# Plain float32 for the memory projection, tokens prepared at twice the pace beside it, and another product order in the first output pair

## The chip, the cores and the metric

One core of one Trainium2 chip runs the whole layer. The metric is device time in microseconds (us) of one execution. Matrix products run on PE (TensorE); DVE is VectorE, ACT ScalarE, POOL GpSimd, SP the engine that issues the DMAs. All code lines report as line 48 (a helper that records every operation), so the rows are told apart by the names of their tiles.

## The reference, cut to what matters

```python
h = rms_norm(x, norm_g[l])                       # x: 512 tokens x 2048
proj = h @ w_in[l]                               # 2048 x 13312: q, k, v, gates, ...
...
mkv = rms_norm(mem, mem_norm_g[l]) @ w_mem_kv[l] # mem: 256 x 2048, w: 2048 x 1024
mk, mv = jnp.split(mkv, 2, axis=-1)
...                                              # three branches, gated and summed
x = x + merged @ w_out[l]                        # 2048 x 2048
```

Everything is float32.

## The kernel before, in words

**Steps.** The program is a list of steps that run_steps (line 120) writes out in order. A step of a projection is one weight chunk of 256 rows by 512 columns. In each turn i, run_steps issues in this order: the loads of step i+6 (on SP), the "adds" of step i (on DVE), the split of step i+2, the products of step i (on PE) with what follows them (post), the work registered for i with at_step, work put off by after, and small tasks with a budget per step. Every engine works its own queue in this order, so an instruction that waits holds up all that stand behind it on its engine.

**The split.** A float32 product is made of three products in the rounded type fp32r: a tile is divided into a high part (ACT casts it) and a low part (DVE subtracts), and products (line 194) adds high by high, high by low and low by high. split_w (line 183) does it for weights. Its buffers are three deep, so the split for step i+2 waits until PE is through with step i-1.

**Memory's projection** (kv_steps, line 409): 16 steps, each two chunk rows by two tiles of 128 memory tokens, 12 products of 512 columns a step. The memory is turned by PE (mem_piece, line 346; 8 transposes a call pair), scaled by DVE, cast by ACT, and POOL makes the low part.

**The tokens** are normed beside those steps: x_norm (line 502) squares four pieces on ACT, makes 1/rms on DVE (with a power on POOL) and scales the pieces on DVE and ACT; x_turn (line 510) turns them on PE and scales them into blocks on DVE.

**Pairs.** Every pair of 512-column slabs after that (pair, line 232) is one Strassen-Winograd product of 2x2 blocks: seven block products P1 to P7 instead of eight, four steps of 12 products each. Their left operands are made once by class Blocks (line 458): copies of blocks (A11, A12, A22), sums of blocks (s1 to s4) and their split forms (S1 to S4). Each of these is one DVE operation of 128x1024 per half, and a split has an ACT cast before it. H are the blocks of the normed tokens (used by the 13 pairs from q on), M those of the merged branches (used by the two output pairs). The right operands are chunks and differences of chunks (sub, line 244, one DVE operation each, in adds). The order is that of line 229: P1, P5, P6, P3, P7, P2, P4. evac (line 253) adds the finished products up on DVE.

Steps 0 to 15 are the memory's, 16 to 43 the q pair's (P1 16 to 19, P5 20 to 23, P6 24 to 27). Before: the tokens' tile t is normed at step 6+3t and turned in the two steps after; A11 is split at 12 and 13, A12 at 18 and 19, s1 to S4 made at 17 to 25, A22 at 29 and 30 (lines 517 to 525). The second to last lines of the schedule (855 to 859) do the same for M, against the first step n_o of the output pair.

Of the kernel before, what the change touches and what calls it, by code (L numbers as in the profile page):

```python
# [65 lines left out]
def trunk_layer(ctx: ExitStack, tc, x, mem, gx, gm, w_in, w_kv, bg, cw, hg, relz, w_a, w_b, w_m, w_o, out):  # L66
# [160 lines left out]


    ORDER = ("P1", "P5", "P6", "P3", "P7", "P2", "P4")
    LEFT = {"P1": "A11", "P5": "S1", "P6": "S2", "P3": "S4", "P7": "S3", "P2": "A12", "P4": "A22"}  # L230

    def pair(name, left, w, done, bias=None):


        n = NK // 2 // KB
        s0 = len(steps)
        raw, ps, cs, st8 = {}, {}, {}, {}
# [15 lines left out]
        def evac(p):  # L253
            b = ps[key[p]]
            new = lambda what: [cell(f"{what}_{name}{t}") for t in range(2)]
            if p == "P1":
                if bias is None:
                    cs["a"] = cs["b"] = new("pa")
                    for t in range(2):
                        ACT.copy(cs["a"][t], b[t])  # L260
                else:
                    cs["a"], cs["b"] = new("pa"), new("pb")
                    for t in range(2):
                        DVE.tensor_tensor(cs["a"][t], b[t], bias_of(0), op=ALU.add)
                        DVE.tensor_tensor(cs["b"][t], b[t], bias_of(1), op=ALU.add)
            if p == "P5":
                cs["f"] = new("pf")
                for t in range(2):
                    DVE.tensor_tensor(cs["f"][t], b[t], cs["b"][t], op=ALU.add)
            if p == "P6":  # L270
                cs["e"] = new("pe") if bias is None else cs["b"]
                for t in range(2):
                    DVE.tensor_tensor(cs["e"][t], b[t], cs["b"][t], op=ALU.add)
            if p == "P3":
                for t in range(2):
                    DVE.tensor_tensor(cs["e"][t], b[t], cs["e"][t], op=ALU.add)
                done(1, 0, cs["e"])
            if p == "P7":
                for t in range(2):
                    DVE.tensor_tensor(cs["f"][t], b[t], cs["f"][t], op=ALU.add)  # L280
                done(1, 2, cs["f"])
            if p == "P2":
                cs["g"] = new("pg")
                for t in range(2):
                    DVE.tensor_tensor(cs["g"][t], b[t], cs["a"][t], op=ALU.add)
                done(0, 0, cs["g"])
            if p == "P4":
                for t in range(2):
                    DVE.tensor_tensor(cs["a"][t], b[t], cs["a"][t], op=ALU.add)
                done(0, 2, cs["a"])  # L290

        for p in ORDER:
            for c in range(n):
                def do_split(p=p, c=c):
                    st8["w", p, c] = split_w(raw[source[p], c], f"{name}_{p}_{c}")

                def mm(p=p, c=c):
                    k = key[p]
                    if k not in ps:
                        ps[k] = [bank(f"ps{k}_{name}_{t}") for t in range(2)]  # L300
                    hi, lo = left(LEFT[p])
                    opens = p in ("P1", "P5", "P6", "P2")

                    def acts(kk, t):
                        kt, ts = c * KB + kk, slice(t * P, (t + 1) * P)
                        return hi[:, kt, ts], lo[:, kt, ts]

                    products(ps[k], st8["w", p, c], acts, opens and c == 0, c == n - 1, not opens)

                st = Step(mm, do_split)  # L310
                if c == n - 1:
                    st.post.append(lambda p=p: evac(p))
                steps.append(st)

        for c in range(n):
            steps[s0 + c].loads.append(loader("11", 0, 0, c))
            steps[s0 + 1 + c].loads.append(loader("12", 0, 1, c))
            steps[s0 + 7 + c].loads.append(loader("22", 1, 1, c))
            steps[s0 + 19 + c].loads.append(loader("21", 1, 0, c))
            steps[s0 + c].adds.append(sub("11", "12", "11", c))  # L320
            steps[s0 + 5 + c].adds.append(sub("11", "22", "11", c))
            steps[s0 + (10, 12, 14, 16)[c]].adds.append(sub("12", "22", "12", c))
            steps[s0 + (20, 21, 22, 24)[c]].adds.append(sub("21", "21", "11", c))
        if bias is not None:
            def load_bias():
# [1 line left out]
            steps[s0].loads.append(load_bias)  # L327


    S_OF = {"A11": (0, 1), "S1": (2, 3), "S2": (4, 5), "S4": (6, 7), "S3": (8, 9), "A12": (10, 11), "A22": (12, 13)}  # L330

    def piece(dst, src, t, j):
        SP.dma_start(dst[:, j, :], src[t * P:(t + 1) * P, j * S:(j + 1) * S])

    SP.dma_start(gm_sb, gm)
    mraw = [slot(t, f"mem{t}") for t in range(NMT)]
    xraw = [slot((13, 9, 8, 6)[t], f"x{t}") for t in range(NT)]
    mT = []

# [5 lines left out]

    def mem_piece(t, k4):
        if not mT:
            for i in range(4):
                mT.append(slot((4, 5, 10, 11)[i], f"mT{i}", (P, 8, MEM), F32R))
        pt = bank(f"pt_mem{t}_{k4}", (P, 4, P))  # L350
        for j in range(4):
            PE.transpose(pt[:, j, :], mraw[t][:, k4, j * P:(j + 1) * P], ident)
        hs = cell(f"hs_mem{t}_{k4}", (P, 4, P))
        DVE.tensor_tensor(hs, pt, gm_sb[:, 4 * k4:4 * k4 + 4].unsqueeze(2).broadcast_to([P, 4, P]), op=ALU.mult)
        i, j, ts = k4 // 2, (k4 % 2) * 4, slice(t * P, (t + 1) * P)
        hi, lo = mT[i][:, j:j + 4, ts], mT[2 + i][:, j:j + 4, ts]
        ACT.copy(hi, hs)
        POOL.tensor_tensor(lo, hs, hi.bitcast(F32), op=ALU.subtract)

    def mem_rstd(t):  # L360
        row_rstd(squares(mraw[t], f"mem{t}"), f"mem{t}", rm[t])

    def act_mem(k, t):
        ts = slice(t * P, (t + 1) * P)
        return mT[k // 8][:, k % 8, ts], mT[2 + k // 8][:, k % 8, ts]


    def heads_out(name, cells, t0, gcol, dst):
# [40 lines left out]
    def kv_steps():  # L409
        st = {"ps": {}}  # L410
        for c in range(NK // KB):
            for half in range(2):
                def do_load(c=c, half=half):
                    st["raw", c, half] = load(w_kv[c * KB * P:(c + 1) * KB * P, half * S:(half + 1) * S], f"kv{half}_{c}")

                def do_split(c=c, half=half):
                    st["w", c, half] = split_w(st["raw", c, half], f"kv{half}_{c}")

                def mm(c=c, half=half):
                    if c == 0:  # L420
                        st["ps"][half] = [bank(f"ps_kv{half}_{t}") for t in range(NMT)]
                    products(st["ps"][half], st["w", c, half], lambda kk, t: act_mem(c * KB + kk, t),
                             c == 0, c == NK // KB - 1)

                s = Step(mm, do_split)
                s.loads.append(do_load)
                if c == NK // KB - 1:
                    def post(half=half):
# [13 lines left out]

    for j in range(1, 4):
        steps[j - 1].loads.append(lambda j=j: first_loads(j))
    steps[3].loads.append(lambda: [SP.dma_start(d, s) for d, s in ((gx_sb, gx), (hg_sb, hg), (cw_sb, cw))])
    for i in range(16):
        steps[4 + 3 * i // 4].loads.append(lambda i=i: piece(xraw[i // 4], x, i // 4, i % 4))

    for k4 in range(4):
        at_step(-3 if k4 == 0 else 2 * k4 - 2, lambda k4=k4: [mem_piece(t, k4) for t in range(NMT)])  # L450
        if k4 == 0:
            at_step(-3, lambda: None)
    for t in range(NMT):
        at_step(8 + t, lambda t=t: mem_rstd(t))
    at_step(5, lambda: DVE.tensor_scalar_mul(qg, hg_sb, float(DH) ** -0.5))


# [39 lines left out]
        def left(self, b):  # L497
            return self.at[b]

    H = Blocks("h", S_OF, {(0, 0): 12, (0, 1): 13, (1, 0): 7, "S12": 9, "S4": 8})  # L500

    def x_norm(t):
        r = row_rstd(squares(xraw[t], f"x{t}"), f"x{t}")
# [11 lines left out]
                          gx_sb[:, 4 * k4:4 * k4 + 4].unsqueeze(2).broadcast_to([P, 4, P]), op=ALU.mult)  # L515

    for t in range(NT):
        b = 6 + 3 * t
        at_step(b, lambda t=t: x_norm(t))
        at_step(b + 1, lambda t=t: [x_turn(t, 0), x_turn(t, 1)])  # L520
        at_step(b + 2, lambda t=t: [x_turn(t, 2), x_turn(t, 3)])
    for i in range(2):
        for n, what in ((12 + i, "A11"), (17, "s1"), (17, "S1"), (19, "s2"), (20, "s4"), (21, "S2"), (22 + i, "S4"),
                        (23, "s3"), (24 + i, "S3"), (18 + i, "A12"), (29 + i, "A22")):
            at_step(n, lambda i=i, what=what: H.do(what, i))

    def w_pair(src, c0, c1=None):
# [286 lines left out]
    def branch(br, n, src, nk, names, first, end):  # L814
# [10 lines left out]
        def done(t, ps):  # L825
# [7 lines left out]
            if end is not None:  # L833
# [3 lines left out]
        steps[s0 + 1].loads.append(get_g)  # L837


    M = Blocks("m", {"A11": (4, 5), "S1": (0, 1), "S2": (12, 13), "S4": (2, 3), "S3": (10, 7), "A12": (9, 8),  # L840
                     "A22": (6, 11)}, {(0, 0): 10, (0, 1): 11, (1, 0): 6, "S12": 7, "S4": 8})

    def m_turn(n, t):
        pt = bank(f"pt_m{n}_{t}", (P, 4, P))
# [7 lines left out]
        branch("m", n, w_m, HM, ("ym",), False, None)  # L852
        branch("b", n, w_b, HB, ("yb0", "yb1"), False, m_turn)
    n_o = len(steps)
    for n, what, i in ((-7, "A11", 0), (-6, "A11", 1), (-2, "s1", 0), (1, "S1", 0), (1, "s1", 1), (1, "S1", 1),
# [3 lines left out]
        at_step(n_o + n, lambda what=what, i=i: M.do(what, i))  # L859


    def out_pair(i):
# [14 lines left out]
                SP.dma_start(xs[half, t], x[t * P:(t + 1) * P, ns])  # L877

        s0 = len(steps)
        pair(f"o{i}", M.left, w_pair(w_o, 2 * S * i), done)  # L880
        for n, args in ((15, (1, 0)), (19, (1, 2)), (23, (0, 0)), (27, (0, 2))):
            steps[s0 + n].loads.append(lambda args=args: get_x(*args))

# [43 lines left out]
```

## Time and profile before

| what | us |
|---|---|
| median of 3 runs (lowest, highest) | 1560.79 (1557.6, 1560.88) |
| the profiled execution's own time | 1558.05 |
| its span, from the first to the last instruction | 1556.3 |
| PE busy | 1487.0 (96%) |
| DVE busy | 1172.2 (75%) |
| ACT busy | 731.0 (47%) |
| mean granted clock of PE | 0.988 of full speed |

All times in the rows are us from the span's start. A matmul's busy time is longer than its distance to the next one, because matmuls overlap; distances of starts are used for sums. "Idle before" stands in square brackets with what ended it.

### The profile page before, as it was taken

The numbers are of one execution on the slowest core, as the hardware profiler recorded it, in microseconds if no ns is written. First come the engines' busy times: TensorE is split into PE (matmuls) and PEld (weight loads), VectorE is DVE, ScalarE is ACT, GpSimd is POOL, SyncE is SP. The second block draws the span as 40 slices with busy tenths as digits, with TensorE's granted clock in tenths as the row PEclk, the third lists the DMA queues.
The fourth block names the chain that finished last, engine by engine and source line by source line (L and its number), as shares of the span: only waits on it lengthen the run. The fifth ranks groups of instructions, "written<-read, shape, count | busy, mean of one in ns | idle before, by whom it ended". The sixth has DMA issues, their size and how long they took to land. (4 is left out here: it accounts for less than half of the span.)

```text
span 1556.3 us, 18174 instructions
## 1 busy us (share of the span) xinstructions
PE 1487.0 (96%) x6760; PEld 1222.1 (79%) x6760; DVE 1172.2 (75%) x1409; ACT 731.0 (47%) x1125; POOL 32.2 (2%) x31
## 2 busy tenths in 40 slices
PE   7868999999999999999999999999898999998998
PEld 6656888888778888788888888888677888877786
DVE  5688777777788887787878787878567455469987
ACT  4855666644435455444353435444366222234442
POOL 2000000000000000000000000000000000000000
PEclk9989999999999999999999999999998999999999
DMA  9513425362425253525252526266654454611633
GB/s 344 181 43 95 149 75 183 95 216 85 126 75 193 89 178 87 157 81 193 97 201 94 203 93 209 83 218 246 203 164 147 152 189 156 208 56 43 214 122 95
DMA packets 125368, 227.18 MB, mean 146 GB/s; under 512 B 9056, under 2 KB 22368, under 8 KB 124512
## 3 DMA queue, kind: packets, MB, share of 16 engines
q1 hardware_dynamic: 125280, 226.02, 44.3%
q8 instruction: 53, 0.87, 0.2%
q14 instruction: 35, 0.29, 0.1%
HBM read 195.58 MB, written 33.03 MB: 147 GB/s over the span
## 5 line engine op out<-in xcount | busy, mean ns | idle before, releaser
L48 ACT CAST whi_o_P<-raw_o 128x1024 fp32r<-128x1024 f32 x56 | 58.7, 1053 | 87.7 <-DVE raw_o L48 20.9
L48 DVE TENSOR_TENSOR wlo_ga_P<-raw_ga,whi_ga_P 128x1024 fp32r<-128x1024 f32 x56 | 68.5, 1224 | 31.2 <-ACT whi_ga_P L48 30.9
L48 ACT CAST whi_ga_P<-raw_ga 128x1024 fp32r<-128x1024 f32 x56 | 58.9, 1052 | 70.1 <-PE psY_ga L48 22.8
L48 ACT CAST whi_gm_P<-raw_gm 128x1024 fp32r<-128x1024 f32 x56 | 58.9, 1052 | 69.2 <-PE psY_gm L48 22.8
L48 ACT CAST whi_gb_P<-raw_gb 128x1024 fp32r<-128x1024 f32 x56 | 58.9, 1052 | 69.2 <-PE psY_gb L48 22.8
L48 DVE TENSOR_TENSOR wlo_gm_P<-raw_gm,whi_gm_P 128x1024 fp32r<-128x1024 f32 x56 | 68.5, 1224 | 29.7 <-ACT whi_gm_P L48 29.6
L48 DVE TENSOR_TENSOR wlo_gb_P<-raw_gb,whi_gb_P 128x1024 fp32r<-128x1024 f32 x56 | 68.5, 1224 | 29.7 <-ACT whi_gb_P L48 28.2
L48 DVE TENSOR_TENSOR wlo_o_P<-raw_o,whi_o_P 128x1024 fp32r<-128x1024 f32 x56 | 68.3, 1223 | 20.1 <-ACT whi_o_P L48 19.9
L48 PE MATMUL ps_wb<-whi_wb,yb_hi 128*128 128x512 f32 x128 | 49.8, 389 | 0.0
L48 PE MATMUL ps_wb<-wlo_wb,yb_hi 128*128 128x512 f32 x128 | 49.8, 389 | 0.0
L48 PE MATMUL ps_wb<-whi_wb,yb_lo 128*128 128x512 f32 x128 | 49.8, 389 | 0.0
L48 ACT CAST whi_cx_P<-raw_cx 128x1024 fp32r<-128x1024 f32 x28 | 29.5, 1055 | 42.4 <-PE psY_cx L48 13.2
L48 DVE TENSOR_TENSOR wlo_cx_P<-raw_cx,whi_cx_P 128x1024 fp32r<-128x1024 f32 x28 | 34.3, 1224 | 18.9 <-ACT whi_cx_P L48 18.6
L48 PE MATMUL ps_kv<-whi_kv,mT 128*128 128x512 f32 x128 | 44.0, 413 | 2.4 <-ACT whi_kv L48 2.4
L48 ACT CAST whi_bz_P<-raw_bz 128x1024 fp32r<-128x1024 f32 x28 | 29.5, 1052 | 33.3 <-PE psZ_bz L48 11.2
L48 DVE TENSOR_TENSOR wlo_mqz_P<-raw_mqz,whi_mqz_P 128x1024 fp32r<-128x1024 f32 x28 | 34.2, 1223 | 14.2 <-ACT whi_mqz_P L48 14.1
L48 ACT CAST whi_mqz_P<-raw_mqz 128x1024 fp32r<-128x1024 f32 x28 | 29.4, 1051 | 31.4 <-PE psZ_mqz L48 10.0
L48 ACT CAST whi_wb<-raw_wb 128x1024 fp32r<-128x1024 f32 x16 | 16.9, 1055 | 58.0 <-DVE g_m L48 17.5
L48 DVE TENSOR_TENSOR wlo_v_P<-raw_v,whi_v_P 128x1024 fp32r<-128x1024 f32 x28 | 34.1, 1222 | 12.9 <-ACT whi_v_P L48 12.7
L48 DVE TENSOR_TENSOR wlo_bz_P<-raw_bz,whi_bz_P 128x1024 fp32r<-128x1024 f32 x28 | 34.2, 1223 | 12.8 <-ACT whi_bz_P L48 12.6
L48 DVE TENSOR_TENSOR wlo_k_P<-raw_k,whi_k_P 128x1024 fp32r<-128x1024 f32 x28 | 34.0, 1222 | 12.2 <-ACT whi_k_P L48 12.1
L48 DVE TENSOR_TENSOR wlo_az_P<-raw_az,whi_az_P 128x1024 fp32r<-128x1024 f32 x28 | 34.1, 1222 | 11.8 <-ACT whi_az_P L48 11.5
(684 smaller groups left out, 4740.5 us busy)
## 6 DMA issues: line engine op xcount, KB each, us to landing
raw_ga<-in_w_in SPq DMA_DIRECT2D x32, 512.0 KB, 4.9
raw_gb<-in_w_in SPq DMA_DIRECT2D x32, 512.0 KB, 5.0
raw_gm<-in_w_in SPq DMA_DIRECT2D x32, 512.0 KB, 5.4
raw_o<-in_w_o SPq DMA_DIRECT2D x32, 512.0 KB, 6.7
raw_kv<-in_w_kv SPq DMA_DIRECT2D x16, 512.0 KB, 8.1
raw_q<-in_w_in SPq DMA_DIRECT2D x16, 512.0 KB, 7.3
raw_k<-in_w_in SPq DMA_DIRECT2D x16, 512.0 KB, 5.0
raw_v<-in_w_in SPq DMA_DIRECT2D x16, 512.0 KB, 4.5
```

The lines of the kernel that those rows point to most:

```text
L48: ins = getattr(self.engine, op)(*args, **kwargs)
```

## The change

Memory's projection leaves out the split: the turned memory is written in float32 by DVE alone, the weights are multiplied as loaded, 4 plain float32 products of 512 columns a step instead of 12 in fp32r. The casts on ACT, the subtractions on DVE and the low parts on POOL of that stage are gone. A weight buffer is now released by PE instead of by the split.

The pieces of x are loaded two a step from step 3 on (before three in four steps from step 4); tile t is normed at step 2+2t and turned at 3+2t and 4+2t. The blocks follow: A11 at 6 and 7, A12 at 8 and 9, s1 at 11, s3 12, S3 13, S1 14, s2 15, s4 16, S4 17 and 18, S2 19 and 20, A22 22 and 23. The squares of the memory move from steps 8 and 9 to 9 and 10. Buffers are laid out anew to fit.

The first output pair takes the products in the order EARLY: P1, P7, P5, P6, P3, P2, P4. S3, which P7 needs, comes from the first two column slabs only. The differences of the right operands and the sums in evac follow; one pair of DVE additions of 128x512 comes on top. The second output pair and the 13 others keep their order.

```diff
+    EARLY = ("P1", "P7", "P5", "P6", "P3", "P2", "P4")
@@ evac
             if p == "P6":
+                cs["e"] = cs["d"] if early else new("pe") if bias is None else cs["b"]
                 for t in range(2):
+                    DVE.tensor_tensor(cs["e"][t], b[t], cs["d" if early else "b"][t], op=ALU.add)
+                if early:
+                    for t in range(2):
+                        DVE.tensor_tensor(cs["f"][t], b[t], cs["f"][t], op=ALU.add)
+                    done(1, 2, cs["f"])
+            if p == "P7" and early:
+                cs["d"] = new("pd")
+                for t in range(2):
+                    DVE.tensor_tensor(cs["d"][t], cs["b"][t], b[t], op=ALU.subtract)
@@ loads and adds of a pair
+            steps[s0 + (2 if early else 7) + c].loads.append(loader("22", 1, 1, c))
+            if early:
+                steps[s0 + 1 + c].adds.append(sub("12", "22", "12", c))
+                steps[s0 + (8, 9, 10, 12)[c]].adds.append(sub("11", "22", "11", c))
+            else:
+                steps[s0 + 5 + c].adds.append(sub("11", "22", "11", c))
+                steps[s0 + (10, 12, 14, 16)[c]].adds.append(sub("12", "22", "12", c))
@@ mem_piece
-        hs = cell(f"hs_mem{t}_{k4}", (P, 4, P))
-        DVE.tensor_tensor(hs, pt, gm_sb[:, 4 * k4:4 * k4 + 4].unsqueeze(2).broadcast_to([P, 4, P]), op=ALU.mult)
...
-        ACT.copy(hi, hs)
-        POOL.tensor_tensor(lo, hs, hi.bitcast(F32), op=ALU.subtract)
+        j = (k4 % 2) * 4
+        DVE.tensor_tensor(mT[k4 // 2][:, j:j + 4, t * P:(t + 1) * P], pt,
+                          gm_sb[:, 4 * k4:4 * k4 + 4].unsqueeze(2).broadcast_to([P, 4, P]), op=ALU.mult)
@@ kv_steps
-                    products(st["ps"][half], st["w", c, half], lambda kk, t: act_mem(c * KB + kk, t),
-                             c == 0, c == NK // KB - 1)
-                s = Step(mm, do_split)
+                    for k in range(c * KB, (c + 1) * KB):
+                        for t, ps in enumerate(st["ps"][half]):
+                            PE.matmul(ps, mT[k // 8][:, k % 8, t * P:(t + 1) * P], st["raw", c, half][:, k % KB, :],
+                                      start=k == 0, stop=k == NK - 1)
+                s = Step(mm)
@@ the schedule beside memory's steps
-        steps[4 + 3 * i // 4].loads.append(lambda i=i: piece(xraw[i // 4], x, i // 4, i % 4))
+        steps[3 + i // 2].loads.append(lambda i=i: piece(xraw[i // 4], x, i // 4, i % 4))
-        at_step(-3 if k4 == 0 else 2 * k4 - 2, lambda k4=k4: [mem_piece(t, k4) for t in range(NMT)])
+        at_step((-3, 0, 3, 5)[k4], lambda k4=k4: [mem_piece(t, k4) for t in range(NMT)])
-        at_step(8 + t, lambda t=t: mem_rstd(t))
+        at_step(9 + t, lambda t=t: mem_rstd(t))
-        b = 6 + 3 * t
+        b = 2 + 2 * t
-        for n, what in ((12 + i, "A11"), (17, "s1"), (17, "S1"), (19, "s2"), (20, "s4"), (21, "S2"), (22 + i, "S4"),
-                        (23, "s3"), (24 + i, "S3"), (18 + i, "A12"), (29 + i, "A22")):
+        for n, what in ((6 + i, "A11"), (8 + i, "A12"), (11, "s1"), (12, "s3"), (13, "S3"), (14, "S1"), (15, "s2"),
+                        (16, "s4"), (17 + i, "S4"), (19 + i, "S2"), (22 + i, "A22")):
@@ the blocks of the output pairs, and the first of these
+    for n, what, i in ((-7, "A11", 0), (-6, "A11", 1), (-2, "s1", 0), (-1, "s3", 0), (1, "s1", 1), (1, "s3", 1),
+                       (0, "S3", 0), (2, "S3", 1), (3, "S1", 0), (4, "S1", 1), (5, "s2", 0), (5, "s2", 1),
+                       (7, "s4", 0), (8, "s4", 1), (9, "S2", 0), (10, "S2", 1),
+                       (12, "S4", 0), (13, "S4", 1), (16, "A12", 0), (17, "A12", 1), (20, "A22", 0), (21, "A22", 1)):
-        pair(f"o{i}", M.left, w_pair(w_o, 2 * S * i), done)
+        pair(f"o{i}", M.left, w_pair(w_o, 2 * S * i), done, order=ORDER if i else EARLY)
```

## Rows read from the trace of the kernel before

**Rows 1.** The page, part 1: busy time, share of the span, instructions.

```profile
PE 1487.0 (96%) x6760; PEld 1222.1 (79%) x6760; DVE 1172.2 (75%) x1409; ACT 731.0 (47%) x1125; POOL 32.2 (2%) x31
```

**Rows 2.** PE's waits, 0 to 72 us: total, times, longest (us).

```profile
PE pt_x L48 <- DVE x L48: 5.6, 2, 4.6
```

**Rows 3.** PE's waits, 72 to 157 us.

```profile
PE psY_q L48 <- DVE wlo_q_P L48: 5.7, 3, 3.9
PE psZ_q L48 <- ACT whi_q_P L48: 5.0, 1, 5.0
PE psZ_q L48 <- DVE wlo_q_P L48: 3.3, 2, 1.8
```

**Rows 4.** PE in order of time: start, busy us; first product of memory, P1, P3, P7.

```profile
9.39 0.79 PE L48 MATMUL ps_kv<-whi_kv,mT 128*128 128x512 f32 x1 [2.38 <-ACT whi_kv L48]
...
72.05 0.39 PE L48 MATMUL psX_q<-whi_q_P,hA_hi 128*128 128x512 f32 x1
...
134.74 0.39 PE L48 MATMUL psZ_q<-whi_q_P,hS_hi 128*128 128x512 f32 x1
...
145.62 0.39 PE L48 MATMUL psY_q<-whi_q_P,hS_hi 128*128 128x512 f32 x1
```

**Rows 5.** Stretches: busy PE, PEld, DVE, ACT, POOL; granted clock; DMA share, GB/s.

```profile
28.00:32.00 4.00, 4.00 (x23) 3.41 (x22) 2.22 (x4) 2.17 (x3) 1.75 (x2) 1.00 1.05 385
...
100.00:104.00 4.00, 3.39 (x8) 2.67 (x9) 4.00 (x5) 4.00 (x9) 0.00 (x0) 0.53 0.00 0
...
1167.00:1177.00 10.00, 10.00 (x72) 8.66 (x71) 6.47 (x25) 7.26 (x24) 0.00 (x0) 1.00 0.02 6
```

**Rows 6.** PE in order of time, attention: one float32 product of 512 columns.

```profile
1164.01 1.02 PE L48 MATMUL psc_b<-k,q 128*128 128x512 f32 x2
1164.87 0.38 PE L48 MATMUL ptp_b<-ident,p_b 128*128 128x128 f32 x2
```

**Rows 7.** PE in order of time, memory's stage: eight transposes and what follows.

```profile
58.18 1.04 PE L48 MATMUL pt_x<-ident,x 128*128 128x128 f32 x8
58.97 0.48 PE L48 MATMUL ps_kv<-whi_kv,mT 128*128 128x512 f32 x1
```

**Rows 8.** Groups of PE's weight loads in attention: busy us, mean ns.

```profile
L48 PEld LDWEIGHTS psc_b<-k,q 128*128 128x128 f32 x64 | 10.3, 202 | 0.1
```

**Rows 9.** DVE in order of time: start, busy us, idle before.

```profile
7.05 0.69 DVE L48 TENSOR_TENSOR hs_mem<-pt_mem,gm_sb 128x512 f32<-128x512 f32 x1 [0.41 <-PE pt_mem L48]
...
36.02 0.16 DVE L48 TENSOR_REDUCE ss_x<-ss_x 128x1 f32<-128x4 f32 x1 [0.93 <-ACT junk L48]
...
37.80 0.88 DVE L48 TENSOR_SCALAR x<-x,r_x 128x512 f32<-128x512 f32 x2
...
85.11 0.16 DVE L48 TENSOR_SCALAR v_mk<-ss_mk 128x8 f32<-128x8 f32 x1
...
87.79 1.22 DVE L48 TENSOR_TENSOR raw_q<-raw_q,raw_q 128x1024 f32<-128x1024 f32 x1
...
91.26 1.22 DVE L48 TENSOR_TENSOR hf_S<-hf,hf 128x1024 f32<-128x1024 f32 x1
...
98.20 1.22 DVE L48 TENSOR_TENSOR raw_q<-raw_q,raw_q 128x1024 f32<-128x1024 f32 x1
```

**Rows 10.** ACT in order of time: the first of a tile's four squares.

```profile
33.00 0.63 ACT L48 ACTIVATE junk<-x 128x512 f32<-128x512 f32 x1
```

**Rows 11.** The chain that ended last, at the first output pair: start, length.

```profile
1388.51 1.22 DVE raw_o L48
...
1444.55 1.14 DVE raw_o L48
1445.69 1.15 DVE wlo_o_P L48
1446.87 5.51 PE psY_o L48 x23
1452.39 10.99 PE psV_o L48 x48
```

More of the change, by code (lines that the diff above doesn't have):

```diff
@@ L229, in trunk_layer, with pair @@
     ORDER = ("P1", "P5", "P6", "P3", "P7", "P2", "P4")
+    EARLY = ("P1", "P7", "P5", "P6", "P3", "P2", "P4")
     LEFT = {"P1": "A11", "P5": "S1", "P6": "S2", "P3": "S4", "P7": "S3", "P2": "A12", "P4": "A22"}
-    def pair(name, left, w, done, bias=None):
+    def pair(name, left, w, done, bias=None, order=ORDER):
+        early = order is EARLY
         n = NK // 2 // KB
@@ L270, in evac @@
             if p == "P6":
-                cs["e"] = new("pe") if bias is None else cs["b"]
+                cs["e"] = cs["d"] if early else new("pe") if bias is None else cs["b"]
                 for t in range(2):
-                    DVE.tensor_tensor(cs["e"][t], b[t], cs["b"][t], op=ALU.add)
+                    DVE.tensor_tensor(cs["e"][t], b[t], cs["d" if early else "b"][t], op=ALU.add)
[3 more added lines that the diff above has]
+                    done(1, 2, cs["f"])
             if p == "P3":
@@ L277, in evac @@
                 done(1, 0, cs["e"])
-            if p == "P7":
+            if p == "P7" and early:
+                cs["d"] = new("pd")
+                for t in range(2):
+                    DVE.tensor_tensor(cs["d"][t], cs["b"][t], b[t], op=ALU.subtract)
+            elif p == "P7":
                 for t in range(2):
@@ L290, in evac @@
                 done(0, 2, cs["a"])
-        for p in ORDER:
+        for p in order:
             for c in range(n):
@@ L301, in mm @@
                     hi, lo = left(LEFT[p])
-                    opens = p in ("P1", "P5", "P6", "P2")
+                    opens = p in ("P1", "P5", "P2", "P7" if early else "P6")
                     def acts(kk, t):
@@ L317, in pair @@
             steps[s0 + 1 + c].loads.append(loader("12", 0, 1, c))
-            steps[s0 + 7 + c].loads.append(loader("22", 1, 1, c))
+            steps[s0 + (2 if early else 7) + c].loads.append(loader("22", 1, 1, c))
             steps[s0 + 19 + c].loads.append(loader("21", 1, 0, c))
             steps[s0 + c].adds.append(sub("11", "12", "11", c))
-            steps[s0 + 5 + c].adds.append(sub("11", "22", "11", c))
-            steps[s0 + (10, 12, 14, 16)[c]].adds.append(sub("12", "22", "12", c))
+            if early:
[4 more added lines that the diff above has]
+                steps[s0 + (10, 12, 14, 16)[c]].adds.append(sub("12", "22", "12", c))
             steps[s0 + (20, 21, 22, 24)[c]].adds.append(sub("21", "21", "11", c))
@@ L327, in pair @@
             steps[s0].loads.append(load_bias)
-    S_OF = {"A11": (0, 1), "S1": (2, 3), "S2": (4, 5), "S4": (6, 7), "S3": (8, 9), "A12": (10, 11), "A22": (12, 13)}
+    S_OF = {"A11": (0, 1), "A12": (10, 11), "S3": (2, 3), "S1": (6, 8), "S4": (7, 12), "S2": (4, 5), "A22": (9, 13)}
     def piece(dst, src, t, j):
@@ L335, in trunk_layer @@
     SP.dma_start(gm_sb, gm)
-    mraw = [slot(t, f"mem{t}") for t in range(NMT)]
+    mraw = [slot(2 + t, f"mem{t}") for t in range(NMT)]
     xraw = [slot((13, 9, 8, 6)[t], f"x{t}") for t in range(NT)]
@@ L347, in mem_piece @@
         if not mT:
-            for i in range(4):
-                mT.append(slot((4, 5, 10, 11)[i], f"mT{i}", (P, 8, MEM), F32R))
+            for i in range(2):
+                mT.append(slot(4 + i, f"mT{i}", (P, 8, MEM)))
         pt = bank(f"pt_mem{t}_{k4}", (P, 4, P))
@@ L352, in mem_piece @@
             PE.transpose(pt[:, j, :], mraw[t][:, k4, j * P:(j + 1) * P], ident)
-        hs = cell(f"hs_mem{t}_{k4}", (P, 4, P))
-        DVE.tensor_tensor(hs, pt, gm_sb[:, 4 * k4:4 * k4 + 4].unsqueeze(2).broadcast_to([P, 4, P]), op=ALU.mult)
-        i, j, ts = k4 // 2, (k4 % 2) * 4, slice(t * P, (t + 1) * P)
-        hi, lo = mT[i][:, j:j + 4, ts], mT[2 + i][:, j:j + 4, ts]
-        ACT.copy(hi, hs)
-        POOL.tensor_tensor(lo, hs, hi.bitcast(F32), op=ALU.subtract)
+        j = (k4 % 2) * 4
+        DVE.tensor_tensor(mT[k4 // 2][:, j:j + 4, t * P:(t + 1) * P], pt,
+                          gm_sb[:, 4 * k4:4 * k4 + 4].unsqueeze(2).broadcast_to([P, 4, P]), op=ALU.mult)
     def mem_rstd(t):
         row_rstd(squares(mraw[t], f"mem{t}"), f"mem{t}", rm[t])
-    def act_mem(k, t):
-        ts = slice(t * P, (t + 1) * P)
-        return mT[k // 8][:, k % 8, ts], mT[2 + k // 8][:, k % 8, ts]
     def heads_out(name, cells, t0, gcol, dst):
@@ L414, in do_load @@
                     st["raw", c, half] = load(w_kv[c * KB * P:(c + 1) * KB * P, half * S:(half + 1) * S], f"kv{half}_{c}")
-                def do_split(c=c, half=half):
-                    st["w", c, half] = split_w(st["raw", c, half], f"kv{half}_{c}")
                 def mm(c=c, half=half):
@@ L444, in trunk_layer @@
         steps[j - 1].loads.append(lambda j=j: first_loads(j))
-    steps[3].loads.append(lambda: [SP.dma_start(d, s) for d, s in ((gx_sb, gx), (hg_sb, hg), (cw_sb, cw))])
+    steps[2].loads.append(lambda: [SP.dma_start(d, s) for d, s in ((gx_sb, gx), (hg_sb, hg), (cw_sb, cw))])
     for i in range(16):
-        steps[4 + 3 * i // 4].loads.append(lambda i=i: piece(xraw[i // 4], x, i // 4, i % 4))
+        steps[3 + i // 2].loads.append(lambda i=i: piece(xraw[i // 4], x, i // 4, i % 4))
     for k4 in range(4):
-        at_step(-3 if k4 == 0 else 2 * k4 - 2, lambda k4=k4: [mem_piece(t, k4) for t in range(NMT)])
-        if k4 == 0:
-            at_step(-3, lambda: None)
+        at_step((-3, 0, 3, 5)[k4], lambda k4=k4: [mem_piece(t, k4) for t in range(NMT)])
     for t in range(NMT):
-        at_step(8 + t, lambda t=t: mem_rstd(t))
+        at_step(9 + t, lambda t=t: mem_rstd(t))
     at_step(5, lambda: DVE.tensor_scalar_mul(qg, hg_sb, float(DH) ** -0.5))
@@ L498, in left @@
             return self.at[b]
-    H = Blocks("h", S_OF, {(0, 0): 12, (0, 1): 13, (1, 0): 7, "S12": 9, "S4": 8})
+    H = Blocks("h", S_OF, {(0, 0): 12, (0, 1): 13, (1, 0): 7, "S12": 9, "S4": 13})
     def x_norm(t):
@@ L837, in branch @@
         steps[s0 + 1].loads.append(get_g)
-    M = Blocks("m", {"A11": (4, 5), "S1": (0, 1), "S2": (12, 13), "S4": (2, 3), "S3": (10, 7), "A12": (9, 8),
-                     "A22": (6, 11)}, {(0, 0): 10, (0, 1): 11, (1, 0): 6, "S12": 7, "S4": 8})
+    M = Blocks("m", {"A11": (4, 5), "S3": (2, 3), "S1": (0, 1), "S2": (12, 13), "S4": (10, 11), "A12": (9, 7),
+                     "A22": (6, 8)}, {(0, 0): 10, (0, 1): 11, (1, 0): 6, "S12": 7, "S4": 8})
     def m_turn(n, t):
@@ L854, in trunk_layer @@
     n_o = len(steps)
-    for n, what, i in ((-7, "A11", 0), (-6, "A11", 1), (-2, "s1", 0), (1, "S1", 0), (1, "s1", 1), (1, "S1", 1),
[3 rows of a table removed]
+    for n, what, i in ((-7, "A11", 0), (-6, "A11", 1), (-2, "s1", 0), (-1, "s3", 0), (1, "s1", 1), (1, "s3", 1),
[3 rows of a table added]
         at_step(n_o + n, lambda what=what, i=i: M.do(what, i))
```

3 rows, old and new, of the table n_o are left out of this document.

## The prediction

> **What bounds the kernel now.** I read the page first: PE is busy 96% of the span [rows 1], so a change counts only where PE waits or where its own work grows. Then PE's waits by stretch. From 157 us to the attention they are few; they lie in two places that this change touches. In memory's stage they are small and come from the tokens' chain on DVE [rows 2]. In the q pair's first three products they are 14.0 us for splits of weights alone [rows 3]; there DVE works without a break (4.00 of 4.00 in [rows 5]), because the tokens' blocks and the weights' splits stand in one queue. Third, PE's starts [rows 4]: the memory's first product is at 9.39, P1 at 72.05, the fourth product (P3) at 134.74, the fifth at 145.62. So a product takes 10.88 undisturbed (2.72 a step, 0.227 a matmul of 512 columns), and P1, P5 and P6, with 32.6 of work, took 62.7. Fourth, the chain that ended last: at the first output pair it runs over DVE from 1388.51 to 1446.87, and over PE after that [rows 11].
>
> **Memory's stage on PE.** Removed: 192 matmuls x 0.227 = 43.6 us. Added: 64 float32 products of 512 columns. The trace has them in attention: start to next start 0.86 us, two passes each [rows 6], at a granted clock of 1.00 where PE is full [rows 5]. 64 x 0.86 = 55.0, so 3.44 a step. The transposes stay: eight cost 0.79 [rows 7], eleven such sets after the first (three of memory, eight of x) cost 8.7. The stage can start when DVE has scaled the first memory pieces, at 7.05 + 0.69 = 7.7 [rows 9], without ACT's cast and split before it (9.39 so far). After a wait of 5.0 [rows 3] the granted clock over 100 to 104 us is 0.53 [rows 5], so PE is at the lower of its two levels (1.2 GHz) for some 4 us, which costs 1.9; I take that once, for the start (0 to 4 is possible). For x's first tile I take a wait of 1.0 (0 to 3): it needs 5.8 MB to be there (memory 2.1, five weight chunks 2.6, itself 1.05), 15 us at the 385 GB/s that the queues reach [rows 5] and some 4 us to start, then 3.0 us of squares on ACT (33.00 to 36.02 [rows 9, 10]) and 2.7 on DVE (36.02 to 38.68 [rows 9]); PE wants it at some 25. Sum: 7.7 + 55.0 + 1.9 + 8.7 + 1.0 = 74.3, against 72.05. On PE the stage alone loses 2.3.
>
> A float32 product loads its weights twice, 202 ns a load [rows 8], well inside a pass of 0.43, so I add nothing for loads. The Trainium skill (TensorE: Matmul & The Clock Gate, Weight-path perf modes) says that the fast weight load is on only where the type isn't FP32, which speaks against the change; by it the loads would come into the open, and the sum would be that of rival 4. That the attention's products follow each other without a gap is against it.
>
> **What hides at nothing.** All of the stage's loads are 14.7 MB, 38 us at 385 GB/s, under 66 us of PE work; a chunk's buffer is now freed by PE and not by the split, so the thirteenth chunk waits for step 0, twelve steps ahead of its use. On SP the pieces of x stand behind their step's chunk and ahead of later chunks, 1 MB a step, 2.7 us, against PE's 3.44; if that cover went, PE would wait the difference. The three small vectors move ahead of one chunk. POOL's eight subtractions had nobody waiting who isn't removed with them. In the output pair the twelve chunks of the three right blocks fill the ring of twelve buffers in both versions; only their order of use changes.
>
> **The tokens beside it, on DVE.** With steps 11 to 15 free of transposes, PE is through with x's last turn at 74.3 - 17.2 = 57.1, and with step 8's at 48.6. DVE then scales two turned pieces (1.4) and norms tile 3 (2.7): 52.6. Now the memory's norms are ahead in the queue: ACT casts a half of A12 (1.0) and makes the squares (3.0) to 56.6; DVE takes 1.8 to 1/rms (36.02 to 37.80), 1.4 for x's pieces, 1.1 for A12: 60.9; the second memory tile's squares are done at 60.6, so 1.8 and 1.4 more: 64.1. PE waits for none of that, but DVE is 7 us behind it.
>
> From 64.1 DVE's list up to the split of step 26 (P6's third chunk) is: 18 operations on blocks (s1, s3, S3, S1, s2, s4, S4, S2, A22, two halves each), 8 differences of chunks, 11 splits, one pair of sums of P5: 38 at 1.14 [rows 11] = 43.3. To that the 1/rms of memory's keys, 2.7 (85.11 to 87.79 [rows 9]), and one wait of 1.3 for ACT, whose evacuation at step 14 stands ahead of its cast of S1. 64.1 + 47.3 = 111.4. Then steps 26 and 27, 5.4: P3 starts at **116.8**, against 134.74: **17.9 us earlier**. PE alone would be there at 74.3 + 32.6 + 0.7 (memory's keys turned) = 107.6, so DVE still limits these products, and that is what is late next: P1's last chunks by 1 to 4 us, the later ones by 0 to 2. From P3 on nothing of the blocks is left in DVE's queue, while before A22's halves stood there and P3 still took its 10.88 [rows 4]; so the gain keeps to the end.
>
> **The first output pair.** DVE is free for it at 1388.51 in both versions [rows 11]. In the order EARLY its list up to the split of step 14 (P6's third chunk) is 13 operations on blocks, 12 differences of chunks, 13 splits and the sums of P7 and P5: 40, so 1388.51 + 45.6 = 1434.1. Two steps of P6 and four of P3 are 16.3: five products end at 1450.4, against 1452.39 (the start of V [rows 11]): **2.0 earlier**. P7 as second product doesn't need the last slab's columns, but its differences come forward too: up to step 5 DVE has three operations more than before; P1's last split is the 7th of the list (1396.5, so P1 ends at 1399.2) and P7's first the 12th (1402.2), a wait of 3. So the order shifts the wait more than it removes it. The added pair of sums (1.3) and the output's sums come after step 15 and leave step 18's split 0.5 us ahead of PE. Ends: 3.4 lost, if the three operations stay in the open; 9.5 gained if DVE limited nothing (63.9 from 1388.51 to 1452.39 less five products of 10.88).
>
> **Sum.** 1558.05 - 17.9 - 2.0 = 1538.1 for the profiled execution. That lies 2.7 under the median of the runs shown; the same gain from the median is 1540.9. I say 1540.
>
> **The rivals.**
> 1. DVE doesn't limit the first three products (casts and sums interleave better, the lists are shorter than I count): P3 at 107.6, 27.1 earlier, with the output pair 1529. For it: ACT loses sixteen casts and DVE sixteen subtractions in that stage. Against it: 38 operations are counted from the code. 0.12.
> 2. The tokens' chain paces memory's stage. In twice the pace a tile has two steps and its transposes, 8.5 us, for sums, norms and a half of a block; where PE waits for it, it is 4.6 [rows 2] and 1.9 for the clock. Two such waits put PE and DVE's list 13 us back: P3 at 129.8, 4.9 earlier, 1551. My steps leave that chain under 1 us of room. 0.16.
> 3. Slower: at the start of the q pair ACT and DVE wait for each other in turn. Before, four operations from 91.26 to 98.20 took 6.94 in place of 4.56 [rows 9], 0.60 each, because every half was summed, cast and subtracted in one go. Were all 38 so, it is 22.8: P3 at 139.6, 4.9 late, and with the output pair 1560.9, 2.9 over the profiled execution. It turns the sign at 0.52 an operation. Against it: sums and splits now stand a step apart. 0.05.
> 4. The change doesn't bring what it says: float32 weights loaded in the open, 128 x 0.202 = 25.9 [rows 8]. The stage ends at 100.2, DVE has caught up by then, P3 at 133.5: 1554.8. 0.04.
>
> **How the numbers follow.** The forecast has 0.63. The range reaches from rival 1's time, 1529, to rival 2's, 1551; beyond it lie half of 1, a third of 2, and 3 and 4, about 0.2. A measurement of this kernel tells 0.2%, 3.1 us, from no change. Faster by more: the forecast, rivals 1 and 2 nearly whole, 0.91. Within: half of 4, some of 2 and 3, 0.05. Slower: 0.04.
>
> **What would show it.** Right: 64 products in 128 records 0.43 apart, P1 at 73 to 76, P3 at 114 to 120, DVE without a break from 64 to 112, PE waiting for splits of q's weights by 1 to 3 us at a time; at the output pair a first wait at P7's first chunk, and the chain still over DVE. Wrong: waits for x over 4 us in memory's stage (2), P3 before 110 (1), idle DVE under ACT's casts (3), passes over 0.43 apart (4), or the fifth output product ending over 4 us from 2.0 earlier.

## The result, and the profile of the changed kernel

The changed kernel takes 1571.14 us in the median, against 1559.19 for the kernel before beside it: a ratio of 1.0077, with a 95% interval of 1.0055 to 1.0099. It is slower by 12, where 20 less were forecast. Yet what the forecast counted did come, and nearly to the microsecond. The loss is made a thousand microseconds later, in code that no hunk of the diff touches. What sets it off is one line of the diff, the new layout of buffers, shown further down.

PE's starts in the changed kernel, in order of time (start, busy us, what; "idle before" and its releaser in brackets):

```profile
8.08 5.24 PE L48 MATMUL ps_kv<-raw_kv,mT 128*128 128x512 f32 x8 [1.37 <-DMA raw_kv<-in_w_kv]
...
57.27 17.33 PE L48 MATMUL ps_kv<-raw_kv,mT 128*128 128x512 f32 x40
74.04 0.80 PE L48 MATMUL psX_q<-whi_q_P,hA_hi 128*128 128x512 f32 x1
...
89.39 0.50 PE L48 MATMUL psX_q<-wlo_q_P,hA_hi 128*128 128x512 f32 x1 [4.20 <-DVE wlo_q_P L48]
...
117.81 0.39 PE L48 MATMUL psZ_q<-whi_q_P,hS_hi 128*128 128x512 f32 x1
...
1094.72 0.80 PE L48 MATMUL psV_gm<-whi_gm_P,hA_hi 128*128 128x512 f32 x1 [15.69 <-ACT whi_gm_P L48]
1095.98 0.80 PE L48 MATMUL psV_gm<-wlo_gm_P,hA_hi 128*128 128x512 f32 x1 [0.46 <-DVE wlo_gm_P L48]
...
1100.28 0.39 PE L48 MATMUL psV_gm<-whi_gm_P,hA_lo 128*128 128x512 f32 x1
...
1119.56 1.46 PE L48 MATMUL psc_b<-k,q 128*128 128x128 f32 x6
1140.42 0.47 PE L48 MATMUL ptp_b<-ident,p_b 128*128 128x128 f32 x1 [19.41 <-ACT p_b L48]
```

The same three late points in the kernel before:

```profile
1095.99 0.39 PE L48 MATMUL psV_gm<-whi_gm_P,hA_hi 128*128 128x512 f32 x1
...
1117.75 1.46 PE L48 MATMUL psc_b<-k,q 128*128 128x128 f32 x6
...
1125.03 0.48 PE L48 MATMUL ptp_b<-ident,p_b 128*128 128x128 f32 x1 [5.82 <-ACT p_b L48]
```

Set side by side, they say where the time came and went:

| moment on PE | before | changed | difference |
|---|---|---|---|
| q pair, P1 starts | 72.05 | 74.04 | +2.0 |
| q pair, P3 starts | 134.74 | 117.81 | -16.9 |
| last gate pair, sixth product (V): could start | 1095.99 | 1079.03 | -17.0 |
| the same: starts | 1095.99 | 1094.72 | -1.3 |
| attention, first scores | 1117.75 | 1119.56 | +1.8 |
| attention, first probabilities turned | 1125.03 | 1140.42 | +15.4 |
| first output pair starts | 1385.03 | 1398.93 | +13.9 |
| second output pair starts | 1474.10 | 1486.92 | +12.8 |
| span | 1556.3 | 1568.6 | +12.3 |

17 us are gained by the third product ("could start" is 1094.72 less the wait of 15.69) and stay gained for 960 us. Two waits then take 29 more than before: 15.7 ahead of the sixth product of the last gate pair, 13.6 more at the attention's first turn. Between them the sixth product takes 1108.67 - 1094.72 = 13.95 in place of 10.88, 3.1 more. One of these is a wait for the low part of its first chunk (the second matmul starts 1.26 after the first, where 0.23 is the undisturbed distance). The other two go to the clock: the next ten matmuls, from 1095.98 to 1100.28, take 4.30 in place of 2.27. The stretches of the changed kernel (columns as in [rows 5]) show the clock: over the wait its mean is 0.73, and for the first matmuls after it 0.50, the lower of its two levels.

```profile
1074.00:1094.00 20.00, 5.03 (x23) 3.83 (x21) 0.00 (x0) 0.38 (x1) 0.00 (x0) 0.73 0.70 268
1094.00:1098.00 4.00, 2.81 (x6) 1.92 (x7) 3.17 (x4) 1.80 (x3) 0.00 (x0) 0.50 1.04 386
```

In the first of these stretches DVE does nothing and ACT one operation: no engine is behind. PE waits for ACT's cast, and ACT for a chunk of weights, which was asked for late:

```profile
1093.62 1.04 ACT L48 CAST whi_gm_P<-raw_gm 128x1024 fp32r<-128x1024 f32 x1 [21.61 <-DMA raw_gm<-in_w_in]
```

Why it was late is to be read from SP, the engine that issues the DMAs. SP in order of time, changed kernel (start, us, what is issued):

```profile
1035.74 0.38 SPq L48 DMA_DIRECT2D k<-k_d  x1
1078.83 0.59 SPq L48 DMA_DIRECT2D v<-v_d  x1
...
1081.62 2.56 SPq L48 DMA_DIRECT2D raw_gm<-in_w_in  x4
...
1094.44 0.42 SPq L48 DMA_DIRECT2D mq<-mq_d  x1
1119.52 0.32 SPq L48 DMA_DIRECT2D mk<-mk_d  x1
...
1123.46 0.59 SPq L48 DMA_DIRECT2D skew<-in_relz  x1
1131.65 0.32 SPq L48 DMA_DIRECT2D bias<-skew  x1
```

and the kernel before:

```profile
1052.87 0.38 SPq L48 DMA_DIRECT2D k<-k_d  x1
1063.31 0.59 SPq L48 DMA_DIRECT2D v<-v_d  x1
...
1075.12 7.45 SPq L48 DMA_DIRECT2D raw_gm<-in_w_in  x4
...
1096.37 0.38 SPq L48 DMA_DIRECT2D mk<-mk_d  x1
...
1109.07 0.59 SPq L48 DMA_DIRECT2D skew<-in_relz  x1
```

Before, v follows k by 10.4 us, in the changed kernel by 43. SP's own waits there (us, times, longest) name the cause, PE's products psY_gm. Third, fifth and seventh product all write a psY_gm; by the starts above, the 42.9 us of v end with the fifth product, and the other wait, some 25 us before the memory's keys (mk), ends with the seventh.

```profile
SPq L48 <- PE psY_gm L48: 67.7, 2, 42.9
```

The code behind it is at lines 675 to 690 of the kernel before, which no hunk touches. During the last gate pair the attention's twelve inputs are fetched into slots 0 to 11, two every four steps, as fast as the pair's products are through with the blocks in them. In the old layout the blocks lie in the slots in the order of the products: A11 in 0 and 1, S1 in 2 and 3, S2 in 4 and 5. The change moves S3 (the fifth product's) to 2 and 3, S1 to 6 and 8, and A22's high part (the last product's) to 9:

```diff
-    S_OF = {"A11": (0, 1), "S1": (2, 3), "S2": (4, 5), "S4": (6, 7), "S3": (8, 9), "A12": (10, 11), "A22": (12, 13)}
+    S_OF = {"A11": (0, 1), "A12": (10, 11), "S3": (2, 3), "S1": (6, 8), "S4": (7, 12), "S2": (4, 5), "A22": (9, 13)}
```

So v's fetch into slot 2 stands on SP until the fifth product ends, with the four chunks of the sixth behind it. The 15.7 us are then the chunk's way: v, z, q and k, 1 MB each, go out ahead of it (1078.83 to 1081.62), its cast starts at 1093.62, and PE follows 1.1 later. The profile's list of transfers has 13.2 us from issue to landing for these four chunks, against 6.6 in the kernel before (1050 to 1100 us). An estimate: 4.7 MB at the 386 GB/s of the second stretch above take 12.2 us, so most of the wait is the four held fetches going out together in front of the chunk.

Later the memory's keys stand for slot 9 until the last product ends, with the first bias behind them. DVE waits 13.8 us for that bias and 5.1 for the second one, whose masked corner it sets before it reads the first scores (DVE's waits from 1119 to 1141 us):

```profile
DVE bias L48 <- DMA bias<-skew: 18.9, 2, 13.8
```

This reading was put to the test.

### The profile page after: what moved, and what is told of

Same layout as the page of the kernel before. It is cut to its first block, busy times and chain, and to the rows that moved or that the text cites. A ratio compares the mean times of both kernels' runs of the same rounds, so it can differ in the third digit from the quotient of the medians.

```text
span 1568.6 us, 17967 instructions
## 1 busy us (share of the span) xinstructions
PE 1492.9 (95%) x6696; PEld 1206.5 (77%) x6696; DVE 1151.5 (73%) x1395; ACT 711.2 (45%) x1101; POOL 22.0 (1%) x23
## 5 line engine op out<-in xcount | busy, mean ns | idle before, releaser
L48 PE MATMUL ps_kv<-raw_kv,mT 128*128 128x512 f32 x128 | 58.2, 606 | 1.4 <-DMA raw_kv<-in_w_kv 1.4
L48 ACT CAST whi_cx_P<-raw_cx 128x1024 fp32r<-128x1024 f32 x28 | 29.5, 1055 | 42.4 <-PE psY_cx L48 13.2
L48 PEld LDWEIGHTS ps_kv<-raw_kv,mT 128*128 128x128 f32 x128 | 24.2, 196 | 28.5 <-issue 26.5
L48 DVE TENSOR_TENSOR wlo_bz_P<-raw_bz,whi_bz_P 128x1024 fp32r<-128x1024 f32 x28 | 34.2, 1222 | 12.8 <-ACT whi_bz_P L48 12.6
L48 ACT CAST whi_wb<-raw_wb 128x1024 fp32r<-128x1024 f32 x16 | 16.9, 1055 | 58.0 <-DVE g_m L48 17.5
L48 DVE TENSOR_TENSOR wlo_k_P<-raw_k,whi_k_P 128x1024 fp32r<-128x1024 f32 x28 | 33.9, 1220 | 12.2 <-ACT whi_k_P L48 12.1
```

Of the source, the lines that this page charges most:

```text
L48: ins = getattr(self.engine, op)(*args, **kwargs)
```

## The experiments

Four kernels ran first. **The fetches in the order of the freed slots**, nothing else changed:

```diff
-        at_step(n_h - 24 + (0, 0, 4, 4, 8, 8, 12, 12, 16, 16, 20, 20)[i], lambda args=args: fetch(*args))
+        at_step(n_h + (-24, -24, -8, -8, -16, -16, -20, -12, -20, 4, -4, -4)[i], lambda args=args: fetch(*args))
```

> The changed kernel, with the twelve fetches for the attention issued in the order in which the new layout frees their slots (v and z of the first heads after the fifth product, the memory's keys after the last one), nothing else. Slot-order theory: both waits come from SP standing at a fetch whose slot is still held, with the chunks of the sixth product and the bias transfers behind it. Then the 15.7 us wait at the last gate pair's sixth product goes to under 1, the 19.4 us wait at the attention's start goes back to 6 or less, and the time is 1571.1 - 15.7 - 13.6 - about 1 for the lower clock after the wait = 1541 (1537 to 1545). Rival, load of the transfers: the chunks come late because more is in flight or the ring of chunk buffers is used otherwise; then both waits stay within 3 us and the time stays at 1566 to 1574.

Measured: 1540.48 us, ratio to the kernel before 0.988 (0.9863 to 0.9897). PE in order of time in that kernel:

```profile
1079.09 0.39 PE L48 MATMUL psV_gm<-whi_gm_P,hA_hi 128*128 128x512 f32 x1
1089.97 0.39 PE L48 MATMUL psY_gm<-whi_gm_P,hA_hi 128*128 128x512 f32 x1
1100.85 1.46 PE L48 MATMUL psc_b<-k,q 128*128 128x128 f32 x6
1108.66 0.47 PE L48 MATMUL ptp_b<-ident,p_b 128*128 128x128 f32 x1 [6.34 <-ACT p_b L48]
```

The sixth product starts without a wait and takes 10.88; the attention's wait is 6.3. The same bytes are moved, by the same ring of buffers, so the amount of load is not the cause; the order of the requests is.

**The same, with the memory's keys left at their old place**, which separates the two waits (the edit is shown against the kernel just above):

```diff
-        at_step(n_h + (-24, -24, -8, -8, -16, -16, -20, -12, -20, 4, -4, -4)[i], lambda args=args: fetch(*args))
+        at_step(n_h + (-24, -24, -8, -8, -16, -16, -20, -12, -20, -8, -4, -4)[i], lambda args=args: fetch(*args))
```

> As the run before, but the memory's keys are fetched at their old place, eight steps before the pairs end, into a slot that the last product still reads. Slot-order theory: the 15.7 us wait at the sixth product is gone, the wait at the attention's start stays at 17 to 21 us, time about 1541 + 13.6 = 1555 (1551 to 1559). If one cause makes both waits, they go or stay together: 1541 or 1571.

Measured: 1552.75 us (one run). PE's waits from 1040 to 1160 us hold one line, and SP issues the memory's keys (mk) when the last product ends, 21 us after the fetch before them:

```profile
PE ptp_b L48 <- ACT p_b L48: 20.8, 3, 19.4
```

```profile
1079.28 0.58 SPq L48 DMA_DIRECT2D z<-z_d  x1
1100.42 0.33 SPq L48 DMA_DIRECT2D mk<-mk_d  x1
...
1104.39 0.60 SPq L48 DMA_DIRECT2D skew<-in_relz  x1
```

One fetch of 0.33 us in SP's queue, put twelve steps earlier, costs 12 us. The two waits are separate.

**The other way round: the kernel before, with v and z of the first heads fetched into the slots of S3.** Nothing of the change is in it.

```diff
-            yield (s + 2, f"v{g}", v_d[:, :, cs], (P, NT, S))
-            yield (s + 3, f"z{g}", z_d[:, :, cs], (P, NT, S))
-        yield (8, "mq", mq_d[:, :, :], (P, 4, S))
-        yield (9, "mk", mk_d[:, :, :], (P, 4, MEM))
+            yield (s + 2 if g else 8, f"v{g}", v_d[:, :, cs], (P, NT, S))
+            yield (s + 3 if g else 9, f"z{g}", z_d[:, :, cs], (P, NT, S))
+        yield (2, "mq", mq_d[:, :, :], (P, 4, S))
+        yield (3, "mk", mk_d[:, :, :], (P, 4, MEM))
```

> The kernel before with two names swapped: the first heads' v and z are fetched into the slots that S3 holds (freed by the fifth product), the memory's queries and keys into those of S1. Nothing of the change is in it. Slot-order theory: a wait of 13 to 18 us before the sixth product of the last gate pair, which the kernel before doesn't have; the attention's start keeps its 6 us or less; time 1572 to 1578. Rival (load of transfers, or something of the change's first stage): no such wait, 1556 to 1562.

Measured: 1577.98 us (one run; the kernel before has 1558.05 beside it). PE's two longest waits from 1040 to 1160 us, and SP's longest from 1030 to 1125:

```profile
PE psV_gm L48 <- ACT whi_gm_P L48: 15.9, 1, 15.9
PE ptp_b L48 <- ACT p_b L48: 6.4, 2, 5.7
```

```profile
SPq L48 <- PE psY_gm L48: 42.9, 1, 42.9
```

The wait of the changed kernel appears in full in a kernel without float32 products, new pace or new order, with the same 42.9 us of SP's, and alone: the attention's wait stays as it was before.

**The new order taken back**, on top of the first of these kernels: ORDER for both output pairs, and the blocks M with their old slots and schedule.

```diff
-        pair(f"o{i}", M.left, w_pair(w_o, 2 * S * i), done, order=ORDER if i else EARLY)
+        pair(f"o{i}", M.left, w_pair(w_o, 2 * S * i), done)
... (slots and schedule of M as in the kernel before)
```

> The first kernel of this call, with the first output pair back in the old order of products (and its blocks' old schedule). From the changed kernel's trace the new order gains 1.7 us up to the sixth product and gives back 0.7 in the seventh: 1 to 2 us slower than the first kernel, 1542 to 1543. If the new order is worth nothing, 0; if it gains what its waits say (9.3 before, 5.1 after, by the three listed groups), 4.

Measured: 1540.10 us, ratio 0.9876 (0.9859 to 0.9893): no difference to 1540.48 that the times can tell. In the traces the first output pair takes 89.10 us (1368.86 to 1457.96) in the old order and 87.99 (1368.13 to 1456.12) in the new, so 1.1 is there. PE's waits from 1360 to 1470 us, new order, then old:

```profile
PE psY_o L48 <- DVE wlo_o_P L48: 5.0, 4, 2.7
PE psX_o L48 <- DVE wlo_o_P L48: 1.2, 1, 1.2
PE psZ_o L48 <- DVE wlo_o_P L48: 0.4, 1, 0.4
```

```profile
PE psZ_o L48 <- DVE wlo_o_P L48: 4.8, 3, 2.0
PE psY_o L48 <- DVE wlo_o_P L48: 4.0, 3, 1.5
```

Both orders wait for DVE's splits, at other products: the wait is shifted, as the prediction said.

Two more kernels ran then. **The kernel before with the float32 projection alone**: mem_piece and kv_steps of the change; old pace, slots and orders.

```diff
-                    products(st["ps"][half], st["w", c, half], lambda kk, t: act_mem(c * KB + kk, t),
-                             c == 0, c == NK // KB - 1)
+                    for k in range(c * KB, (c + 1) * KB):
+                        for t, ps in enumerate(st["ps"][half]):
+                            PE.matmul(ps, mT[k // 8][:, k % 8, t * P:(t + 1) * P], st["raw", c, half][:, k % KB, :],
+                                      start=k == 0, stop=k == NK - 1)
... (no split in these steps; mem_piece as in the change)
```

> The kernel before with nothing but the memory's projection in plain float32: old pace of the tokens and blocks, old slots, old orders. Theory: the products themselves cost PE 11.4 us more and give ACT and DVE time that they don't need in that stage; the q pair's first products stay behind DVE's list of blocks, which is as long and starts as late as before. P3 starts at 134 to 139 us (134.74 before) and the time is 1556 to 1563, no gain. Rival: the casts and subtractions that are gone are what held the q pair back; then P3 starts before 127 and the time is under 1551.

Measured: 1559.21 us, against 1556.86 for the kernel before beside it, ratio 1.0012 (1.0002 to 1.0022); P3 at 135.34. The float32 product on its own gains nothing and may lose 2 us: ACT and DVE get time where they didn't lack it. The longest waits of the q pair are still those of [rows 3]:

```profile
PE psY_q L48 <- DVE wlo_q_P L48: 5.7, 3, 3.9
PE psZ_q L48 <- ACT whi_q_P L48: 5.0, 1, 5.0
```

So the 17 us don't come from the float32 products by themselves; what is left in that stage is the earlier tokens and blocks. Whether these could be had with the old split products was not tried: the turned memory's low parts take two more slots, and the new schedule has A12 in them from step 8 on.

**The first two biases loaded earlier**, on top of the first kernel, since its largest wait was then the attention's 6.3 us:

```diff
-        DVE.memset(bias[0:64, S - 64:], NEG)
...
+    for k in range(2):
+        at_step(n_h - 6 + 3 * k, lambda k=k: bias_h.update({k: bias_of(k)}))
...
-                    for k in ((0, 1) if h == 0 else (h + 1,)):
-                        if k < HB:
-                            bias_h[k] = bias_of(k)
+                    if h and h + 1 < HB:
+                        bias_h[h + 1] = bias_of(h + 1)
+                    DVE.memset(bias_h[h][0:64, S - 64:], NEG)
```

> The changed kernel with the fetches in the order of the freed slots, and now the first two heads' biases loaded six and three steps before the attention, their masked corner set where the head begins. If the 6.3 us wait at the attention's start is the way of the first bias through two transfers that begin too late on SP, it goes to under 2.5 us and with the lower clock after it 4 to 6 us are gained: 1534 to 1537. If it is ACT's or DVE's work on the first scores, or the v and z fetches, nothing changes: 1538 to 1542. If the two buffers that the biases hold are missed by the last gate pair, splits or sums there wait and it is slower: over 1543.

Measured: 1533.31 us, ratio 0.9842 (0.9824 to 0.986), the fastest of all; the wait shrinks to 2.0. It is 7 under the first kernel in the times and in the spans (1537.9 and 1530.9), but 6 by the ratios, as the kernel before had 1556.86 beside this run: the upper end of what was expected, or a little more. The edit loads the biases earlier and also takes the second bias's corner out from in front of the first scores; the run doesn't tell the two apart. PE in order of time, this kernel and then the first:

```profile
1104.06 0.33 PE L48 MATMUL ptp_b<-ident,p_b 128*128 128x128 f32 x1 [1.95 <-ACT p_b L48]
1104.23 1.02 PE L48 MATMUL psc_b<-k,q 128*128 128x512 f32 x2
1105.09 0.38 PE L48 MATMUL ptp_b<-ident,p_b 128*128 128x128 f32 x2
...
1109.31 1.02 PE L48 MATMUL psc_b<-k,q 128*128 128x512 f32 x2
```

```profile
1108.92 1.91 PE L48 MATMUL psc_b<-k,q 128*128 128x512 f32 x2
1110.63 0.64 PE L48 MATMUL ptp_b<-ident,p_b 128*128 128x128 f32 x2
...
1116.66 1.02 PE L48 MATMUL psc_b<-k,q 128*128 128x512 f32 x2
```

At the first turn it is 1108.66 - 1104.06 = 4.6 ahead; at the same scores of the second head 1116.66 - 1109.31 = 7.35. Between them lies, for the most part, the clock: a float32 product of 512 columns takes 0.86 after the short wait and 1.71 after the long one, and the granted clock is 1.00 from 1104 to 1108 us in this kernel and 0.50 from 1108 to 1112 us in the first.

## Why the prediction was right in its terms and wrong in its sum

**The stage on PE** was right: P1 at 74.04, forecast 74.3. That it is off by only 0.3 is in part luck. The stage starts at 8.08 (7.7), the 64 products take 56.3 (55.0 and 1.9 for the clock), the eleven sets of transposes 9.65 (8.7), and the wait of 1.0 for x isn't there. The first four products take 1.7 more than four later ones, near the 1.9 set down for the clock; but the granted clock reads 1.00 from 8 to 14 us, so this trace doesn't show the clock as their cause. Five steps free of transposes take 74.04 - 57.27 = 16.8, so a float32 product of 512 columns has 0.84, two passes of 0.42. Rival 4 falls with it: the loads of the stage's weights took 193 ns each, inside a pass. The rule of the Trainium skill named there (TensorE: Matmul & The Clock Gate, Weight-path perf modes) may hold, but no run here shows slower loads for float32: the fp32r weights of the same stage took 198 ns a load in the kernel before.

**DVE's list** was right: it ends the tokens' last block at 63.4 (forecast 64.1), and P3 starts at 117.81 (forecast 116.8, so 1.0 late). The waits stand where they were put, at P1's last chunks (1.5 and 4.2 us) and at one later chunk (1.1). DVE is not quite without a break, busy 43.4 of the 48 us from 64 to 112. Of its waits there, 1.3 us are for ACT's casts of chunks, which the list didn't have; they are of the size by which P3 comes late, but that they are its cause isn't shown. Rivals 1, 2 and 3 didn't come about: PE waits for no tile of x in the changed kernel's stage. One reading behind this term was too narrow: the 14.0 us of [rows 3] are not all of PE's waits from 72 to 157 us. Two more groups stand in the same view of the kernel before, and the first of them, a wait for the tokens' last tile, is gone in the changed kernel:

```profile
PE pt_x L48 <- DVE x L48: 4.4, 1, 4.4
PE psX_q L48 <- DVE wlo_q_P L48: 1.4, 1, 1.4
```

**The first output pair** was right, and in its parts: five products end 1.7 earlier, counted from the pair's start (forecast 2.0), and PE waits 2.8 at P7's first chunk (forecast 3). The seventh product then gives 0.7 back, so the pair as a whole gains 1.1.

**What failed is the step "What hides at nothing"**, with the sentence that ends DVE's step, "so the gain keeps to the end". That step went through the loads of the changed stage and SP's queue there, but took the new layout of slots as free. A slot is a resource with later users: the fetches for the attention, which wait for it in SP's queue. This term, put at nothing, measured 15.7 + 3.1 + 13.6 = 32.4. Less the 17.0 gained that is the +15.4 of the table; 1.5 of it comes back in the attention, the first output pair takes off its 1.1, and the span ends at +12.3. No rival held it: all of mine lay in the stages that the change rewrites. The range, built from bounds on the counted terms, could not reach a term that wasn't among them. The kernel with the fetches put in order has 1540.48, the time that the counted terms alone had given (1540).

It could have been seen blind. The fetch loop names slots 0 to 11 and steps n_h - 24 to n_h - 4; beside the two lines of S_OF, that gives for every fetch the product it waits for: before, always the one just ended; after, the fifth for slots 2 and 3, at step n_h - 20, and the seventh for slot 9. Behind v's fetch stand the sixth product's chunks, whose loads are due from n_h - 15 on. They could go out only when the fifth product was over, so the four held fetches, a whole transfer, a cast and a split had to lie open on PE. [Rows 4] to [rows 11] showed none of this, since in the kernel before the two orders agreed and no chunk came late there.

## What to carry to other kernels

A layout is a schedule. When a change renames buffers, list for every renamed buffer who takes it next, when that request is issued, what frees it now, and what stands behind the request in its queue; a request issued before its buffer is free stops everything behind it in its queue, however short it is itself, as v's fetch did here (42.9 us). And when a change gives less than its own stage shows, subtract the two traces moment by moment: a difference that holds for 960 us and then jumps points to the place.

## What the runs showed that had not been expected

Fetches that take 0.33 and 0.59 us of SP's time cost 12 and 16 us, while PE, DVE and ACT stood almost idle together; on such a stretch the lists of the busy engines don't name the cause, and SP's waits do. PE's lower clock after a wait adds to it, 2.0 us at the sixth product. And of the three edits two are worth nothing by themselves that the times can tell: the float32 products alone cost 0.1%, and taking the new order back changes nothing clear of noise. What is left for the 1.2% that the first of these kernels gains is the pace, for which the float32 products free the slots; that is a subtraction, since the pace alone was not run.
